# Half-wise layer norms, a whole-float32 router and idle TensorE products in a two-layer hybrid transformer kernel

## The chip, the cores and the metric

The kernel runs on one core of one Trainium2 chip. The time is the device time of one execution in microseconds (us), as a median of timed runs. Engines are called as in the profile: PE (TensorE matmul), PEld (its weight load), DVE (VectorE), ACT (ScalarE), POOL (GpSimd), SP (SyncE, which issues most DMAs).

## The reference

256 tokens of 1024 float32 features run through two layers. Each adds three branches in turn, with a layer norm after each; the cut below leaves the mixer and the attention to their names.

```python
x = layer_norm(x, ln_in_g, ln_in_b)
for l in range(2):
    h = hybrid_mixer(x, w_in[l], ...)            # retention and an RWKV7 scan, gated, w_out
    x = layer_norm(ALPHA * x + h, ln1_g[l], ln1_b[l])
    h = memory_cross_attention(x, mem, xa_wq[l], xa_wkv[l], xa_wo[l])
    x = layer_norm(ALPHA * x + h, ln2_g[l], ln2_b[l])
    h = grouped_moe(x, router_w, router_bias, moe_w_gate[l], moe_w_up[l], moe_w_down[l])
    x = layer_norm(ALPHA * x + h, ln3_g[l], ln3_b[l])

def grouped_moe(...):   # 16 experts in 4 groups of 4, width 512
    affinity = sigmoid(t @ router_w)
    choice = affinity + router_bias
    group_score = sum(top_k(choice by group, 2))
    best_group = argmax(group_score)
    idx = top_k(choice inside best_group, 2)
    wts = affinity[idx] / sum(affinity[idx])
    y = sum over e of combine[:, e] * ((silu(t @ w_gate[e]) * (t @ w_up[e])) @ w_down[e])
```

## The kernel before

All weights stream from memory in pieces of 1 MB on SP's queue into a ring of buffers (`slot`, `fetch`, `take`); a piece is loaded when its buffer's last reader is done. A Tile scheduler puts the instructions of each engine in an order once, when the program is built; `behind(ins)` asks for instructions to be issued after `ins`. Products of the dense parts take float32 numbers as a high and a low half: `split` (L135, L136) rounds the high one on ACT and subtracts the low one on DVE. `mm` (L127) is a product, `tr` (L131) a transpose on PE. The names in rows: `x` the tokens, `xT` their split transposes, `wh` the split weights, `raw`, `A`, `x` and `wh` the ring's buffers, `memT` the transposed memory tokens, `tp`, `acc`, `g` and `rk` PSUM tiles.

`layer_norm` (L284 to L301) takes statistics of both token blocks, finds the inverse root by three Newton steps on tiny tiles (L287 to L294), and writes x in halves of 512 features: subtract and scale (L297) for four pieces, then the last scale and offset (L301) for the same four. The transposes that follow on PE read x by columns of both blocks. In layer 0 the norm of the mixer and that of the attention have products on the memory tokens beside them (`spill_keys`, `spill_values`); in layer 1 those were done earlier, and PE has no other work there.

The expert part (`moe`) transposes x, splits it into `rx` (two buffers of `wh`), and `route` multiplies it with the split router as the stationary side (`g<-rx,rw`), copies to `big`, sums the halves with small products, and chooses experts in sixteen small DVE operations, from `aff` (L1048) to `sel` (L1075). Products with `sel` rank the tokens. `xs` is the split x for the gather, which multiplies it with a one-hot `oh`: half of the column blocks, then transposes of `oh` (`ohT`) and weights (`cws`), then the other half. Products of `xs` with a unit matrix start the output sums (`y`). An overflow flag is made from `rank` ahead of the gather. The expert stage then runs eight pairs of experts: gate, up, down.

## Time and profile before

| | |
|---|---|
| timed runs | 1311.02, 1313.77, 1318.09 us; median 1313.77 us |
| profiled execution | 1306.93 us, span 1304.6 us |
| PE busy | 1207.4 us (93%), 7648 instructions |
| DVE busy | 681.2 us (52%), 1446 instructions |
| ACT busy | 424.4 us (33%) |
| POOL busy | 81.9 us (6%) |
| HBM traffic | 253 GB/s over the span |

The shares are averages over stages with different limits. Layer 0 runs to about 673 us: norm and mixer, attention, router (404 to 452), experts (452 to 673). Layer 1 follows: mixer, its norm (965 to 986), attention, its norm (1041 to 1052), router and gather (1052 to 1072), experts (1072 to 1290), last norm. What a stage is worth is read from who ends PE's waits in it, and from the clock that PE was granted there.

### The profile page before, as it was taken

How to read it: one execution, taken by the hardware profiler on the slowest of the kernel's cores; microseconds unless marked ns; L12 is line 12 of the kernel's file. 1: busy time of each engine (PE TensorE's matmuls, PEld its weight loads, DVE VectorE, ACT ScalarE, POOL GpSimd, SP SyncE). 2: the span in 40 equal slices, each digit the busy share in tenths (PEclk: the TensorE clock that was granted, in tenths of full speed). 3: DMA queues.
4: the chain of work that ended last, by engine and by line, in shares of the span. 5: the costliest groups of instructions: out<-in, count | busy, mean ns of one | idle time of the engine just before them, and what ended most of it. 6: DMA issues, size and time to landing. Idle time of an engine off the chain costs nothing. (4 is left out here: it accounts for less than half of the span.)

```text
span 1304.6 us, 19215 instructions
## 1 busy us (share of the span) xinstructions
PE 1207.4 (93%) x7648; PEld 853.0 (65%) x7648; DVE 681.2 (52%) x1446; ACT 424.4 (33%) x689; POOL 81.9 (6%) x157
## 2 busy tenths in 40 slices
PE   8999998998999999999879999989979969999995
PEld 7887787996988744433339876879959744443332
DVE  6589787777548411101046797876875561110114
ACT  4556433453544301100025664234534220110000
POOL 0022222000000000000000113220000000000000
PEclk9999989999999999999999999899989979999998
DMA  9746222298635899999987453131987349999994
GB/s 324 260 143 192 79 75 76 81 372 283 232 129 207 310 396 403 399 395 402 400 331 229 155 182 106 43 108 66 346 295 282 109 162 382 400 396 400 402 396 200
DMA packets 189838, 331.04 MB, mean 254 GB/s; under 512 B 23152, under 2 KB 80880, under 8 KB 188720
## 3 DMA queue, kind: packets, MB, share of 16 engines
q1 hardware_dynamic: 187728, 324.51, 69.0%
q10 hardware_dynamic: 1728, 3.15, 0.7%
q0 software_dynamic: 288, 2.10, 0.4%
q8 instruction: 63, 1.03, 0.3%
q14 instruction: 31, 0.25, 0.1%
HBM read 321.86 MB, written 7.87 MB: 253 GB/s over the span
## 5 line engine op out<-in xcount | busy, mean ns | idle before, releaser
L136 DVE TENSOR_TENSOR wh<-raw,wh 128x1024 fp32r<-128x1024 f32 (+1 forms) x204 | 233.4, 1148 | 122.2 <-ACT wh L135 120.4
L135 ACT CAST wh<-raw 128x1024 fp32r<-128x1024 f32 (+1 forms) x204 | 199.8, 980 | 181.3 <-PE acc L127 166.5
L127 PE MATMUL acc<-xT,wh 128*128 128x256 f32 x1824 | 246.0, 290 | 2.3 <-DVE xT L136 1.5
L127 PEld LDWEIGHTS acc<-xT,wh 128*128 128x128 f32 x1824 | 228.5, 193 | 6.8 <-issue 2.1
L127 PE MATMUL g<-raw,xe 128*64 128x512 f32 x688 | 176.9, 596 | 1.4 <-DMA raw<-in_moe_w_up_dram 1.4
L127 PEld LDWEIGHTS g<-raw,xe 128*64 128x64 f32 x688 | 53.3, 137 | 95.4 <-issue 90.8
L127 PE MATMUL acc<-wh,xT 128*128 128x512 f32 x384 | 99.9, 405 | 2.7 <-DVE vg L557 2.7
L127 PE MATMUL g<-raw,hT 128*64 128x512 f32 x352 | 97.0, 596 | 1.8 <-DMA raw<-in_moe_w_down_dram 1.2
L1159 DVE TENSOR_TENSOR act<-act,g 128x512 f32<-128x512 f32 x16 | 11.0, 688 | 157.9 <-PE g L127 157.9
L1275 ACT ACTIVATE yh<-g,ws 128x512 fp32r<-128x512 f32 x32 | 22.0, 688 | 198.7 <-PE g L127 198.7
L1276 DVE SCALAR_TENSOR_TENSOR yl<-g,ws,yh 128x512 fp32r<-128x512 f32 x32 | 24.0, 751 | 114.6 <-ACT yh L1275 113.5
L127 PEld LDWEIGHTS acc<-wh,xT 128*128 128x128 f32 x384 | 70.2, 188 | 19.7 <-DVE vg L557 3.5
L127 PEld LDWEIGHTS g<-raw,hT 128*64 128x64 f32 x352 | 30.2, 137 | 55.5 <-issue 49.0
L127 PE MATMUL g<-wh,xe 128*64 128x512 f32 x184 | 56.5, 597 | 3.2 <-DMA wh<-in_moe_w_up_dram 3.2
L1206 DVE COPY xe<-g 128x512 f32<-128x512 f32 x16 | 11.1, 692 | 82.8 <-PE g L127 82.8
L127 PE MATMUL acc<-wh,memT 128*128 128x512 f32 x192 | 50.5, 414 | 0.3 <-ACT memT L135 0.3
L1147 ACT ACTIVATE act<-g 128x512 f32<-128x512 f32 x16 | 9.6, 598 | 124.9 <-PE g L127 124.9
L127 PE MATMUL acc<-memT,wh 128*128 128x256 f32 x384 | 46.9, 284 | 1.1 <-DVE wh L136 0.7
L127 PEld LDWEIGHTS acc<-memT,wh 128*128 128x128 f32 x384 | 46.3, 191 | 1.9 <-DVE wh L136 0.9
L127 PE MATMUL acc<-wh,mT 128*128 128x512 f32 x192 | 45.9, 398 | 0.8 <-DVE xr L406 0.7
L127 PE MATMUL acc<-wh,oT 128*128 128x512 f32 x192 | 45.7, 395 | 1.0 <-DVE x L406 0.8
L127 PE MATMUL acc<-ys,wh 128*128 128x256 f32 x384 | 45.1, 280 | 0.0
(292 smaller groups left out, 1691.3 us busy)
## 6 DMA issues: line engine op xcount, KB each, us to landing
raw<-in_w_in_dram SPq DMA_DIRECT2D x46, 1024.0 KB, 5.3
raw<-in_moe_w_down_dram SPq DMA_DIRECT2D x44, 1024.0 KB, 15.4
raw<-in_moe_w_gate_dram SPq DMA_DIRECT2D x43, 1024.0 KB, 13.9
raw<-in_moe_w_up_dram SPq DMA_DIRECT2D x43, 1024.0 KB, 13.9
raw<-in_xa_wkv_dram SPq DMA_DIRECT2D x16, 1024.0 KB, 10.1
wh<-in_moe_w_up_dram SPq DMA_DIRECT2D x15, 1024.0 KB, 14.2
A<-in_moe_w_down_dram SPq DMA_DIRECT2D x10, 1024.0 KB, 13.7
A<-in_moe_w_gate_dram SPq DMA_DIRECT2D x9, 1024.0 KB, 13.8
```

What stands on the lines that cost most here:

```text
L127: self.nc.tensor.matmul(out, lhsT, rhs, start=start, stop=stop, skip_group_check=True)
L135: self.nc.scalar.copy(out=hi, in_=src)
L136: (eng or self.nc.vector).tensor_sub(out=lo, in0=src, in1=hi)
L1147: nc.scalar.activation(act, ps, AF.Silu)
L1159: nc.vector.tensor_mul(out=act, in0=act, in1=ps)
L1206: nc.vector.tensor_copy(out=flat(t), in_=flat(ps))
L1275: nc.scalar.activation(yh, y[jc], AF.Copy, scale=ws)
L1276: nc.vector.scalar_tensor_tensor(out=yl, in0=y[jc], scalar=ws, in1=yh, op0=OP.mult, op1=OP.subtract)
```

## The change

- `layer_norm`: the first half of x gets its first scale before the Newton steps and its last scale right after them; the second half's first scales stand behind the first half's.
- `idle`: products of the unit matrix with constants, read by nobody, 10 behind w_out's last product in layer 1, 8 behind wo's in the last layer, 4 behind the logits there.
- In layer 1 the low halves of the first query weight piece are subtracted on POOL; those of the next two pieces stand behind the norm.
- Router: the transposed x is kept in whole float32 (`rx`, one buffer of `wh`), is the stationary side, and meets the whole router in sixteen products of 16 columns (eight blocks of features, two of tokens), straight into `z`. The choice takes twelve DVE operations.
- `xs` is split behind the last copy of `rx`, ahead of `aff`; the `y` products stand behind the logits.
- First gather: all column blocks first; transposes and weights of the lists behind the first gate product; the overflow flag (`beyond`) after the columns.

```diff
+W_NORM1, W_NORM2, W_ROUTE = 10, 8, 4
...
-    c["tie"] = np.broadcast_to((np.arange(4)[None] < np.arange(4)[:, None]).reshape(1, 16), (128, 16))
+    c["tie"] = np.broadcast_to((np.arange(4)[None] < np.arange(4)[:, None]).reshape(1, 16) * -1.2e-38, (128, 16))
...
-        self.nc.tensor.matmul(out, lhsT, rhs, start=start, stop=stop, skip_group_check=True)
+        self.product = self.nc.tensor.matmul(out, lhsT, rhs, start=start, stop=stop, skip_group_check=True)
+
+    def idle(self, n):
+
+        ps = self.pp.tile([128, 384], F32, name="warm", tag="b", bufs=4)
+        with self.behind(self.product):
+            for _ in range(n):
+                self.nc.tensor.matmul(ps, self.c["ident"], self.cst[:, 0:384], start=True, stop=True, skip_group_check=True)
...
-            self.split(flat(raw[:, j * n:j * n + n, :]), flat(hi), flat(lo))
+            self.split(flat(raw[:, j * n:j * n + n, :]), flat(hi), flat(lo), self.lower)
...
-            nc.vector.scalar_tensor_tensor(out=y, in0=e, scalar=1.5, in1=y, op0=OP.add, op1=OP.mult)
+            self.normed = nc.vector.scalar_tensor_tensor(out=y, in0=e, scalar=1.5, in1=y, op0=OP.add, op1=OP.mult)
+
         for j, s in enumerate(half):
             for tb in range(2):
-                nc.vector.scalar_tensor_tensor(out=out[:, tb, s], in0=src(tb, j), scalar=mv[:, tb, 0:1], in1=gb[:, 0, s],
-                                               op0=OP.subtract, op1=OP.mult)
-        for j, s in enumerate(half):
+                with self.behind(self.normed) if j else ExitStack():
+                    nc.vector.scalar_tensor_tensor(out=out[:, tb, s], in0=src(tb, j), scalar=mv[:, tb, 0:1], in1=gb[:, 0, s],
+                                                   op0=OP.subtract, op1=OP.mult)
             for tb in range(2):
                 self.normed = nc.vector.scalar_tensor_tensor(out=out[:, tb, s], in0=out[:, tb, s], scalar=y[:, tb], in1=gb[:, 1, s],
                                                              op0=OP.mult, op1=OP.add)
...
-            self.rw = const.tile([128, DK, 2, NE], F32R, name="rw")
+            self.rw = const.tile([128, DK, NE], F32, name="rw")
...
-            rwf = self.small.tile([128, DK, NE], F32, name="rwf", bufs=1)
-            nc.sync.dma_start(out=rwf, in_=a["router"])
-            self.split(rwf, self.rw[:, :, 0, :], self.rw[:, :, 1, :])
+            nc.sync.dma_start(out=self.rw, in_=a["router"])
...
         gb = self.project(a["w_out"][l], mT, xr, a["ln1_g"][l], a["ln1_b"][l])
+        if l:
+            self.idle(W_NORM1)
...
         for j in range(4):
-            with self.behind(normed) if j < NQ else ExitStack():
+
+            self.lower = nc.gpsimd if l and j == 0 else None
+            with self.behind(normed) if l and 0 < j < 3 else ExitStack():
                 ps = self.col(a["xa_wq"][l], j * 256, xT)
...
         gb = self.project(a["xa_wo"][l], oT, x, a["ln2_g"][l], a["ln2_b"][l])
+        if l + 1 == self.layers:
+            self.idle(W_NORM2)
         self.layer_norm(lambda tb, j: x[:, tb, j * 512:j * 512 + 512], gb, x)
...
-    def route(self, xT, rp, mo, lp):
+    def route(self, z, rp, mo):
...
-        ps = self.pp.tile([2 * NE, 256], F32, name="g", tag="b", bufs=4)
-        for k in range(DK):
-            w = self.rw[:, k].rearrange("p a e -> p (a e)")
-            for i in range(2):
-                self.mm(ps, w, xT[k // 2][i][:, k % 2, :], k == 0 and i == 0, k == DK - 1 and i == 1)
...
-        lg = big[0:2 * NE, 0:256]
-        nc.vector.tensor_copy(out=lg, in_=ps)
-        z = self.pp.tile([128, 2, NE], F32, name="g", tag="b", bufs=4)
-        for tb in range(2):
-            self.mm(z[:, tb, :], lg[:, tb * 128:tb * 128 + 128], c["id16"][0:2 * NE], True, True)
...
+        def ahead(v, n, at, count):
+            d = big[:, at:at + 16 * n].rearrange("p (a b c) -> p a b c", a=n, b=4)
+            nc.vector.tensor_tensor(out=d, in0=v[:, :, None, :].to_broadcast([128, n, 4, 4]), in1=v[:, :, :, None].to_broadcast([128, n, 4, 4]), op=OP.subtract)
+            nc.vector.scalar_tensor_tensor(out=d, in0=d, scalar=1.0, in1=tie.to_broadcast([128, n, 4, 4]), op0=OP.mult, op1=OP.is_gt)
+            nc.vector.tensor_reduce(out=count, in_=d, axis=AX.X, op=OP.add)
...
-        gt, eq = (big[:, i:i + 128].rearrange("p (a b c) -> p a b c", a=8, b=4) for i in (256, 384))
-        cj, ci = c4[:, :, None, :].to_broadcast([128, 8, 4, 4]), c4[:, :, :, None].to_broadcast([128, 8, 4, 4])
-        nc.vector.tensor_tensor(out=gt, in0=cj, in1=ci, op=OP.is_gt)
-        nc.vector.tensor_tensor(out=eq, in0=cj, in1=ci, op=OP.is_equal)
-        tie = c["tie"].rearrange("p (i j) -> p i j", i=4)[:, None, :, :].to_broadcast([128, 8, 4, 4])
-        nc.vector.tensor_mul(out=eq, in0=eq, in1=tie)
-        nc.vector.tensor_add(out=gt, in0=gt, in1=eq)
         before = R("before", (128, 8, 4))
-        nc.vector.tensor_reduce(out=before, in_=gt, axis=AX.X, op=OP.add)
+        ahead(c4, 8, 0, before)
...
-        m, best, top = R("m", (128, 2)), R("best", (128, 2, 4)), R("top", (128, 2))
-        nc.vector.tensor_reduce(out=m, in_=score, axis=AX.X, op=OP.max)
-        nc.vector.tensor_tensor(out=best, in0=score, in1=m[:, :, None].to_broadcast([128, 2, 4]), op=OP.is_equal)
-        nc.vector.tensor_mul(out=best, in0=best, in1=c["desc"][:, None, :].to_broadcast([128, 2, 4]))
-        nc.vector.tensor_reduce(out=top, in_=best, axis=AX.X, op=OP.max)
-        nc.vector.tensor_tensor(out=best, in0=best, in1=top[:, :, None].to_broadcast([128, 2, 4]), op=OP.is_equal)
+        ahead(score, 2, 128, worse)
...
+        return rank, cws, cw
+
+    def beyond(self, rank, cw, rp, lp):
...
-                rx = []
+                rx = self.wpool.tile([128, DK, 256], F32, name="rx", tag="wh", bufs=self.nhi)
+                z = self.pp.tile([128, 2, NE], F32, name="g", tag="b", bufs=4)
+
+                def logits(k):
+                    for i in range(k, k + 2):
+                        for tb in range(2):
+                            self.mm(z[:, tb, :], rx[:, i, tb * 128:tb * 128 + 128], self.rw[:, i, :], i == 0 and tb == 0, i == DK - 1)
+
                 for k in range(0, DK, 2):
                     ps = self.pp.tile([128, 2, 2, 128], F32, name="g", tag="b", bufs=4)
                     for j in range(2):
                         for tb in range(2):
                             self.tr(ps[:, j, tb, :], x[:, tb, (k + j) * 128:(k + j + 1) * 128])
-                    if k % 4 == 0:
-                        t = self.wpool.tile([128, 2, 2, 2, 256], F32R, name="rx", tag="wh", bufs=self.nhi)
-                    rx.append([t[:, k // 2 % 2, i] for i in range(2)])
-                    self.split(flat(ps), flat(rx[-1][0]), flat(rx[-1][1]))
-                rank, cws, cover, flag = self.route(rx, rp, mo, self.small)
-            xs = [self.xt.tile([128, 2, D], F32R, name=f"xs{i}", tag=f"xT{i}") for i in range(2)]
-            for tb in range(2):
-                self.split(x[:, tb, :], xs[0][:, tb, :], xs[1][:, tb, :])
-            if l + 1 < self.layers:
-                self.spill_values(l + 1, mem, 0)
-            self.ring = self.ring + [(self.wpool, "wh", self.nhi)] * self.nhi + [(self.xp, "x", 1)] + ([(self.aux, "A", 2)] * 2 if l + 1 < self.layers else [])
-            py.append([self.pp.tile([128, 512], F32, name="y", tag="c", bufs=2) for _ in range(2)])
-            for tb in range(2):
-                for jc in range(2):
-                    for i in range(2):
-                        self.mm(py[tb][jc], self.identr, xs[i][:, tb, jc * 512:jc * 512 + 512], i == 0, False)
-            lists, acts, ys = {}, {}, {}
-            step = self.gather(mo, 0, xs, rank, cws, lists)
-            self.finish(step)
+                    if k < DK // 2:
+                        nc.scalar.copy(out=flat(rx[:, k:k + 2, :]), in_=flat(ps))
+                    else:
+                        turned = nc.vector.tensor_copy(out=flat(rx[:, k:k + 2, :]), in_=flat(ps))
+                    if k >= 4:
+                        logits(k - 4)
+                logits(DK - 4)
+                logits(DK - 2)
+                chosen = self.product
+                if l + 1 == self.layers:
+                    self.idle(W_ROUTE)
+                xs = [self.xt.tile([128, 2, D], F32R, name=f"xs{i}", tag=f"xT{i}") for i in range(2)]
+                with self.behind(turned):
+                    for tb in range(2):
+                        self.split(x[:, tb, :], xs[0][:, tb, :], xs[1][:, tb, :])
+                rank, cws, cw = self.route(z, rp, mo)
+                if l + 1 < self.layers:
+                    self.spill_values(l + 1, mem, 0)
+                self.ring = self.ring + [(self.wpool, "wh", self.nhi)] * self.nhi + [(self.xp, "x", 1)] + ([(self.aux, "A", 2)] * 2 if l + 1 < self.layers else [])
+                py.append([self.pp.tile([128, 512], F32, name="y", tag="c", bufs=2) for _ in range(2)])
+                with self.behind(chosen):
+                    for tb in range(2):
+                        for jc in range(2):
+                            for i in range(2):
+                                self.mm(py[tb][jc], self.identr, xs[i][:, tb, jc * 512:jc * 512 + 512], i == 0, False)
+                lists, acts, ys = {}, {}, {}
+                first = self.gather(mo, 0, xs, rank, cws, lists)
+                next(first)
+                cover, flag = self.beyond(rank, cw, rp, self.small)
...
+                    if p == 0:
+                        self.finish(first)
...
-        for k in range(0, DK - 4, 2):
+        for k in range(0, DK - 4 if g else DK, 2):
             columns(k)
+            if g:
+                yield
+        if not g:
+            lists[g] = [xe, None, None]
             yield
...
-        for k in range(DK - 4, DK, 2):
+        for k in range(DK - 4 if g else DK, DK, 2):
             columns(k)
```

VectorE at the first norm of layer 1; `raw_8973` is a piece of wq, `lnm` the mean, `lny` and `lne` Newton's tiles. Before:

```order
L136 TENSOR_TENSOR wh<-raw_8973,wh 128x1024
L285 BN_AGGR lnm<-lnst 128x2
L297 SCALAR_TENSOR_TENSOR x<-xr,lnm,raw 128x512
L287 TENSOR_SCALAR lnv<-lnm 128x2
L297 SCALAR_TENSOR_TENSOR x<-xr,lnm,raw 128x512
L288 TENSOR_SCALAR lni<-lnv 128x2
L290 TENSOR_SCALAR lnn<-lnv 128x2
L297 SCALAR_TENSOR_TENSOR x<-xr,lnm,raw 128x512
L289 TENSOR_SCALAR lny<-lni 128x2
L297 SCALAR_TENSOR_TENSOR x<-xr,lnm,raw 128x512
L293 SCALAR_TENSOR_TENSOR lne<-lny,lnn 128x1 x2
```

And now, from the last Newton steps on:

```order
L301 SCALAR_TENSOR_TENSOR lny<-lne,lny 128x2
L300 SCALAR_TENSOR_TENSOR lne<-lny,lnn 128x1 x2
L301 SCALAR_TENSOR_TENSOR lny<-lne,lny 128x2
L309 SCALAR_TENSOR_TENSOR x<-x,lny,raw 128x512 x2
L306 SCALAR_TENSOR_TENSOR x<-xr,lnm,raw 128x512 x2
L309 SCALAR_TENSOR_TENSOR x<-x,lny,raw 128x512 x2
L143 TENSOR_TENSOR xT_8978<-tp,xT_8977 128x512 x2
L143 TENSOR_TENSOR wh<-raw_8966,wh 128x1024
```

The split of wq left the place ahead of the first scale; of the four first scales (L297, now L306) two stand between the last scales (L309) of the halves, and a split of wq follows the first split of xT.

TensorE from the attention's last product to the router's products in layer 1 (`oT` is the attention's output; L131 is now L138). Before:

```order
L127 MATMUL acc<-wh,oT_9300 128x512
L131 MATMUL g<-cst,x 128x128 x16
L127 MATMUL y<-xs_9644,identr 128x512
L127 MATMUL y<-xs_9645,identr 128x512
L127 MATMUL y<-xs_9644,identr 128x512
L127 MATMUL y<-xs_9645,identr 128x512
L127 MATMUL g<-rx,rw 32x256 x9
L127 MATMUL y<-xs_9644,identr 128x512
L127 MATMUL g<-rx,rw 32x256 x4
L127 MATMUL y<-xs_9644,identr 128x512
L127 MATMUL g<-rx,rw 32x256 x3
```

And now:

```order
L134 MATMUL warm<-cst 128x384 x8
L138 MATMUL g<-cst,x 128x128 x9
L127 MATMUL g<-rw,rx 128x16 x4
L138 MATMUL g<-cst,x 128x128
L127 MATMUL g<-rw,rx 128x16 x4
L138 MATMUL g<-cst,x 128x128 x6
L127 MATMUL g<-rw,rx 128x16 x8
L134 MATMUL warm<-cst 128x384 x4
L127 MATMUL y<-xs_9589,identr 128x512
```

Idle products (`warm`) came in ahead of the transposes and behind the logits, logits stand among the transposes, and the `y` products moved behind them.

TensorE inside the first gather of layer 1 (`raw_9699`, `raw_9701` are pieces of the experts' gate weights). Before:

```order
L127 MATMUL g<-oh,xs_9644 128x256 x2
L127 MATMUL g<-oh,xs_9645 128x256 x2
L131 MATMUL g<-cst,oh 128x128 x4
L127 MATMUL g<-cws,oh 64x2 x8
L127 MATMUL g<-oh,xs_9644 128x256 x2
L127 MATMUL g<-oh,xs_9645 128x256 x2
```

And now, at the end of the gather's columns:

```order
L127 MATMUL g<-oh,xs_9589 128x256 x2
L127 MATMUL g<-oh,xs_9590 128x256 x2
L127 MATMUL g<-ones,ovc 1x1
L127 MATMUL g<-raw_9699,xe 64x512
L127 MATMUL g<-raw_9701,xe 64x512
```

The transposes of `oh` and the products with `cws` left the middle of the gather; the flag's product (`ovc`) is followed at once by the gate products.

## Rows read from the trace of the kernel before

**Rows 1.** Windows: window and length (us), busy us (instructions) by engine, granted clock, DMA share, GB/s.
```profile
296.00:328.00 32.00, 27.38 (x120) 21.52 (x120) 22.95 (x42) 11.32 (x15) 0.00 (x0) 0.95 0.82 280
404.00:452.00 48.00, 47.80 (x348) 43.06 (x350) 32.30 (x74) 20.61 (x28) 0.00 (x0) 1.00 0.75 267
452.00:673.00 221.00, 215.76 (x1018) 84.58 (x1014) 29.96 (x45) 23.05 (x36) 0.00 (x0) 1.00 1.03 396
...
965.00:986.00 21.00, 12.38 (x76) 10.72 (x74) 14.99 (x34) 5.11 (x8) 0.00 (x0) 0.76 0.85 307
1041.00:1052.00 11.00, 3.97 (x18) 3.10 (x17) 10.27 (x28) 1.70 (x3) 0.00 (x0) 0.69 0.00 1
1052.00:1072.00 20.00, 13.89 (x95) 11.95 (x95) 10.72 (x36) 4.74 (x10) 0.00 (x0) 0.74 0.69 263
1072.00:1290.00 218.00, 213.47 (x1016) 84.06 (x1017) 29.32 (x45) 22.05 (x34) 0.00 (x0) 1.00 0.99 381
```

**Rows 2.** Timeline of PE at the start: start, length (us), instruction, count, [idle before, releaser].
```profile
24.95 11.43 PE L127 MATMUL acc<-memT,wh 128*128 128x256 f32 x94 [0.69 <-DVE wh L136]
...
43.70 2.50 PE L127 MATMUL acc<-xT,wh 128*128 128x256 f32 x19 [1.50 <-DVE xT L136]
```

**Rows 3.** Timeline of DVE at the same place.
```profile
41.67 0.17 DVE L458 TENSOR_SCALAR rest<-vec 128x4 f32<-128x4 f32 x1 [2.87 <-DMA vec<-in_vecs_dram]
```

**Rows 4.** Timeline of PE beside the first norm of layer 0.
```profile
314.40 0.90 PE L131 MATMUL tp<-cst,sg 128*128 128x128 f32 x4 [4.21 <-DVE memT L136]
```

**Rows 5.** Timeline of DVE at the same place.
```profile
313.66 0.68 DVE L136 TENSOR_TENSOR memT<-tp,memT 128x512 fp32r<-128x512 f32 x1
```

**Rows 6.** Timeline of PE after the first norm of layer 1.
```profile
974.33 2.20 PE L131 MATMUL tp<-cst,x 128*128 128x128 f32 x8 [8.59 <-DVE x L301]
...
985.97 1.99 PE L127 MATMUL rk<-kT,qT 128*128 128x256 f32 x8
```

**Rows 7.** Timeline of DVE in the first norm of layer 1.
```profile
964.05 1.23 DVE L136 TENSOR_TENSOR wh<-raw,wh 128x1024 fp32r<-128x1024 f32 x1 [1.57 <-ACT wh L135]
...
967.70 1.17 DVE L136 TENSOR_TENSOR wh<-raw,wh 128x1024 fp32r<-128x1024 f32 x1
...
970.39 0.75 DVE L297 SCALAR_TENSOR_TENSOR x<-xr,lnm,raw 128x512 f32<-128x512 f32 x1
```

**Rows 8.** Timeline of PE from the second norm of layer 1 to the experts.
```profile
1049.00 3.51 PE L131 MATMUL g<-cst,x 128*128 128x128 f32 x16 [7.03 <-DVE x L301]
...
1061.85 0.58 PE L127 MATMUL g<-sel,cst 128*128 128x16 f32 x2 [4.38 <-DVE sel L1075]
1062.26 0.59 PE L127 MATMUL g<-sel,ones 128*128 128x16 f32 x2
...
1064.88 3.78 PE L127 MATMUL g<-oh,xs 128*128 128x256 f32 x16
...
1071.92 2.37 PE L127 MATMUL g<-raw,xe 128*64 128x512 f32 x10
```

**Rows 9.** Timeline of DVE at the same place.
```profile
1048.19 2.74 DVE L301 SCALAR_TENSOR_TENSOR x<-x,lny,raw 128x512 f32<-128x512 f32 x4
...
1054.91 1.22 DVE L136 TENSOR_TENSOR xs<-x,xs 128x1024 fp32r<-128x1024 f32 x1
...
1057.73 0.18 DVE L1048 TENSOR_SCALAR aff<-aff 128x32 f32<-128x32 f32 x1 [1.28 <-ACT aff L1047]
```

**Rows 10.** Timeline of SP, the DMA queue, as the experts of layer 1 begin.
```profile
1075.60 0.88 SPq L150 DMA_DIRECT2D raw<-in_moe_w_down_dram  x2
```

**Rows 11.** Windows, as rows 1, of stretches granted half the clock.
```profile
830.09:840.33 10.24, 8.93 (x40) 8.73 (x41) 9.06 (x20) 2.96 (x3) 0.92 (x2) 0.50 0.20 33
...
1058.78:1069.02 10.24, 5.69 (x27) 5.60 (x28) 4.79 (x25) 0.81 (x2) 0.00 (x0) 0.50 0.72 287
```

**Rows 12.** One tile, `rm`: count, shortest/median/longest ns, first and last start, forms.
```profile
L569 DVE TENSOR_TENSOR rm<-rq,mixc x8: 426/928/962, 124.6 to 817.1; 128x256 f32<-128x256 f32 x8
```

**Rows 13.** Groups of POOL's instructions: busy us, mean ns, idle before and releasers.
```profile
L863 POOL TENSOR_TENSOR bkc<-bk,P 128x512 f32<-128x512 f32 x8 | 8.7, 1089 | 28.1 <-DVE bk L844 15.6 <-PE rk L131 12.3
```

More of the change, by code (lines that the diff above doesn't have):

```diff
@@ L34 @@
 NEXTRA = 4
-NQ = 0
 NM = 1
@@ L78, in _constants @@
     c["id64"] = np.concatenate([np.eye(64), np.eye(64)], 0)
-    c["id16"] = np.concatenate([np.eye(16)] * 8, 0)
-    c["desc"] = np.broadcast_to(np.arange(4, 0, -1)[None], (128, 4))
     gam = np.log(1.0 - 2.0 ** (-5.0 - np.arange(4.0)))
@@ L96, in pack @@
         return np.ascontiguousarray(np.concatenate([np.asarray(c[k], np.float32) for k in names], 1)), off
-    always = ["ident", "tri", "i64", "id16", "id64", "desc", "tie"]
+    always = ["ident", "tri", "i64", "id64", "tie"]
     return pack(always), pack([k for k in c if k not in always])
@@ L119, in __init__ @@
         self.ahead = []
+        self.lower = None
     def tap(self, name, ap):
@@ L1052, in route @@
         self.tap("choice", ch)
[L1054 to L1061 removed]
+        tie = c["tie"].rearrange("p (i j) -> p i j", i=4)[:, None, :, :]
+        def ahead(v, n, at, count):
[3 more added lines that the diff above has]
+            nc.vector.tensor_reduce(out=count, in_=d, axis=AX.X, op=OP.add)
+        c4 = ch.rearrange("p b (g e) -> p (b g) e", e=4)
         before = R("before", (128, 8, 4))
[L1063 removed]
+        ahead(c4, 8, 0, before)
         two, score = R("two", (128, 8, 4)), R("score", (128, 2, 4))
@@ L1066, in route @@
         nc.vector.tensor_reduce(out=score.rearrange("p b g -> p (b g)"), in_=two, axis=AX.X, op=OP.add)
-        m, best, top = R("m", (128, 2)), R("best", (128, 2, 4)), R("top", (128, 2))
-        nc.vector.tensor_reduce(out=m, in_=score, axis=AX.X, op=OP.max)
-        nc.vector.tensor_tensor(out=best, in0=score, in1=m[:, :, None].to_broadcast([128, 2, 4]), op=OP.is_equal)
-        nc.vector.tensor_mul(out=best, in0=best, in1=c["desc"][:, None, :].to_broadcast([128, 2, 4]))
-        nc.vector.tensor_reduce(out=top, in_=best, axis=AX.X, op=OP.max)
-        nc.vector.tensor_tensor(out=best, in0=best, in1=top[:, :, None].to_broadcast([128, 2, 4]), op=OP.is_equal)
+        worse = R("worse", (128, 2, 4))
+        ahead(score, 2, 128, worse)
         sel = R("sel")
         nc.vector.scalar_tensor_tensor(out=sel.rearrange("p b (g e) -> p (b g) e", e=4), in0=before, scalar=1.5,
-                                       in1=best.rearrange("p b g -> p (b g)")[:, :, None].to_broadcast([128, 8, 4]),
-                                       op0=OP.is_lt, op1=OP.mult)
+                                       in1=worse.rearrange("p b g -> p (b g)")[:, :, None].to_broadcast([128, 8, 4]),
+                                       op0=OP.is_lt, op1=OP.is_gt)
         rank = R("rank", pool=mo)
@@ L1093, in route, with R @@
         self.split(cw, cws[:, :, :, 0], cws[:, :, :, 1])
+        return rank, cws, cw
+    def beyond(self, rank, cw, rp, lp):
+        nc = self.nc
+        def R(name, shape=(128, 2, NE), pool=rp):
+            return pool.tile(list(shape), F32, name=name, bufs=1)
         over, ovc = R("over"), R("ovc", (128, 1))
@@ L1103, in route @@
         nc.vector.tensor_mul(out=cover, in0=over, in1=cw)
-        return rank, cws, cover, flag
+        return cover, flag
     def moe(self, l, x, mem):
```

## Prediction

> **What bounds the kernel now.** I read the table of stretches first [rows 1]. TensorE (PE) is busy for 47.80 of 48 us in the first router and for nearly all of both expert stages, where the weight stream also fills the DMA engines (share 1.03 and 0.99). An edit there moves nothing unless it takes work from PE or bytes from the stream. The second layer is different around its norms: from 965 to 986 PE is busy for 12.38 of 21 us, from 1041 to 1052 for 3.97 of 11, from 1052 to 1072 for 13.89 of 20. In these stretches the granted clock is a mean of 0.76, 0.69 and 0.74, so some 5.0, 3.4 and 5.2 us are lost to it on top of the standing still (twice those lengths were granted 1.2 GHz of 2.4). The reader should then look at who ends PE's waits: the layer norm's scale on VectorE (DVE) for 8.59 and 7.03 us [rows 6, 8], the choice of experts on DVE for 4.38 us [rows 8]. In layer 0 PE waits 4.21 us in its first layer norm, for a split of the memory tokens that queues behind the norm on DVE [rows 4, 5]. These waits are what the change can win: the four stretches.
>
> **The start.** The changed order puts the first tokens' transposes and their splits ahead of the two small operations on `vec`, which today hold DVE for 2.87 us until a DMA lands at 41.67 [rows 3]; the last splits of x run behind them and PE waits 1.50 us for them, after a gap of 0.69 us earlier [rows 2]. The 1.50 should go, and most of the 0.69, which stands where transposes now come earlier: I take -2.0. The bounds are 0 (the next weight piece is late instead) and -2.2, the sum of the two.
>
> **First norm of layer 0.** Before, all four subtract-and-scale operations (0.75 us each) stand on DVE ahead of Newton's steps, and the memory's split reaches DVE at 313.66 only [rows 5]. Now two of the four stand behind Newton, so the split can start about 2 x 0.75 = 1.5 us earlier and PE's wait falls from 4.21 to some 2.5 us: -1.7. PE then works through to the next transposes, so this is passed on. The mean clock of 0.95 over 32 us is 3.4 us at 1.2 GHz, which cost 1.7 us [rows 1]; it follows this wait and may vanish with it. Bounds -1.7 and -3.4; I take -2.7, nearer the second half, since the wait is cut by 40%. Five more splits of weights stand behind the second norm of this layer; products on memory tokens hide it, as PE at 47.80 of 48 us shows. Without that cover each would cost up to its 1.2 us.
>
> **Router and experts of layer 0.** The sixteen logits products are whole float32 and cost PE more than the sixteen they replace: a whole float32 product shows as two records. Those with `sel`, 16 columns wide, started 1061.85 and 1062.26, 0.41 apart at the low clock [rows 8], so about 0.21 at full: 16 x 0.21 = 3.4 us, against 16 x 0.12 = 1.9 (94 split products in 11.43 us [rows 2]), that is +1.5. Moving the lists' transposes and weights (four and sixteen products, about 1.4 us) behind the first gate product only shifts them. The expert stage has 221 - 215.8 = 5.2 us of PE waits and a full weight stream, which absorb 1.5: I take 0, the bound is +1.5.
>
> **First norm of layer 1.** Three things leave DVE ahead of the first transposes: a split of wq of 1.17 us in the middle of the norm, now behind it, and two of the four first scales, 2 x 0.75 [rows 7]. Half of these lie in the shadow of Newton's dependent small steps, as two of the four rows do today; so 1.17 + 0.6, about -1.7, gives the first transposes at 972.6 instead of 974.33. The second half of x is written about 1.1 us earlier too. The ten idle products stand between w_out and the transposes. Each has 384 columns of float32; four products of 256 columns (eight records) took 1.99 us [rows 6], 0.43 each with the last one's end taken off, so 1.5 x 0.43 = 0.65 us, together 6.5 us; the gap left is about 7, so they fit and delay nothing while the clock is full. If the clock then holds, the first query projection, which began at 1.2 GHz and ended at 985.97, ends at about 982.5: -3.5. If it doesn't, -1.7. A price the other way: wq's first piece is now split on GpSimd, two of 128x1024. Nearest rows: 1.09 us for 128x512 there, so 2.2 each [rows 13]. From when the cast is ready, before the DVE split at 964.05, they end by about 967, before the scales start. I take -2.75, since some of the clock or of GpSimd's time may bite. DVE slows beside GpSimd: one multiply of 128x256 took 426 ns at its shortest and a median of 928 [rows 12].
> [...]
>
> **Second norm and router of layer 1.** PE's transposes start at 1049.00 after 7.03 us [rows 8]; with two scales fewer ahead they start 1.1 to 1.4 us earlier, but x's second half is written as late as before, so only the logits count. DVE now copies two column pairs instead of subtracting four; the copy of `big` and PE's four summing products go. But both subtractions for `xs` (1.22 us each [rows 9]) move ahead of the first operation on `aff`, and whoever waits for `aff` waits for them. x ends at 1050.93 (1048.19 + 2.74 [rows 9]); seven transposes of 0.11 (half of 3.51 / 16 [rows 8]) and two copies of 0.7 (as long as the splits of [rows 5]) bring the last copy to 1052.7 or so. Two subtractions behind it end at 1055.1, if ScalarE's two casts were done by then; if they too wait for the last copy, each about as long as a subtraction, at 1056.2. The operation on `aff` follows there, against 1057.73: -1.5 to -2.6, I take -2.1. The sixteen operations from `aff` to `sel` span 1057.73 to 1061.85, 0.26 each; twelve remain: -1.0. Between `sel` and the first gather product the overflow flag's chain goes, -0.4. That is -3.5 without any help of the clock. Today the clock is at 1.2 GHz from 1058.78 to 1069.02 [rows 11], after PE stood still. Held at full, the three products with `sel` (six records, 0.21 apart) save 0.6. The first gate product follows the first gather product by 1071.92 - 1064.88 = 7.04 us; its first 16 gather products take 3.78 at the low clock, 0.22 each [rows 8]. Now 32 come first and the lists later: 32 x 0.22 = 7.0 at the low clock, 32 x 0.12 = 3.8 at full. So -3.5 with the clock lost, -3.5 - 0.6 - 3.2 = -7.3 with it held. The four idle products after the logits last 2.6 us, the y products 1.9; then PE still waits some 2 us for `sel` and 1 us for the one-hot. I take -5.25: clock lost in this wait, back within the gather.
> SP issues its next weights at 1075.60, after the first gate products have read their pieces [rows 10], and no bytes move from 1041 to 1052 [rows 1]. The stream, full from there (0.99), starts earlier by what the gate gains, and the end with it.
>
> **Last norm.** Two scales now stand behind Newton's steps, whose gaps they used to fill: +0.3 (0 to +0.6).
>
> **Sum.** -2.0 - 2.7 - 2.75 - 5.25 + 0.3 = -12.4 on the profiled 1306.93 us (span 1304.6), so 1294.5. That run is 6.8 us under the median of the three timed runs, 1313.77; I apply the same difference there: 1301.4.
>
> **Rivals.**
> *Clock not held.* The idle products fail to keep the full clock and only the order pays: -2.0 - 1.7 - 1.7 - 3.5 + 0.3 = -8.6, 1305.2. For it: ten products follow w_out, but DVE is what PE waits for, and a wait of 2 to 3 us after `sel` is left. Against: the other three waits shrink.
> *Held everywhere.* -2.0 - 3.4 - 3.5 - 7.3 + 0.3 = -15.9, 1297.9.
> *GpSimd in the way.* If a scale on DVE waits for a whole GpSimd split of 2.2 us in the first norm of layer 1 [rows 12, 13], the forecast gives that back: 1303.6. For it: the multiply at 928 ns. Against: the GpSimd splits have nearly ended when the two-input scales begin.
> *The stream sets the ends.* If the expert stages end when the weights do whenever PE starts, what is won ahead of them is swallowed: only +0.3 is left, 1314. For it: DMA shares of 1.03 and 0.99. Against: the stream stands still before the gate and restarts with it.
> *Slower: the scan's clock.* In the RWKV scan of each layer PE works in pieces of 64 columns with DVE in between, and one stretch of 10.24 us each was granted 1.2 GHz (830.09 to 840.33: PE busy 8.93, DVE 9.06) [rows 11]. Such a stretch costs up to 5.1 us. All of it starts earlier now and meets other pauses; three more stretches undo -12.4, four give +8.1 on the median, 1321.9. For it: the scan is DVE-paced. Against: its order is unchanged and only one stretch in each layer fell so far.
>
> **How the numbers follow.** Forecast 0.50, held everywhere 0.13, clock not held 0.17, GpSimd in the way 0.07, the stream 0.08, slower 0.05. The range takes the forecast's own bounds (route -3.5 to -7.3, start 0 to -2.2), both clock cases and GpSimd in the way: 1294 to 1311, leaving out the stream, the slower case and a tail below. Half a percent, 6.6 us, is about what a measurement of this kernel can tell from no change, so faster means under 1307.2: nearly all of the forecast and the held clock, two thirds of the clock lost, most of GpSimd in the way: 0.76. Same 0.19, slower 0.05.
>
> **What would show it.** In the changed profile: PE idle for 1.50 before the last x products gone; the wait for the memory's split at 2.5 us; the transposes after the first norm of layer 1 some 7.0 us after w_out's last product, granted clock 965 to 986 near 1; the first gate product 5 us earlier beyond the earlier shifts, counted from wo's last product (before: 1041.97 to 1071.92); SP's restart as much earlier. I am wrong if the expert stages lengthen by what the parts ahead of them gain, if idle products run into the transposes' start, or if a new stretch at 1.2 GHz appears.

## The result and the profile after

The changed kernel took 1296.46 us (median of four runs, 1293.89 to 1300.92) against 1312.39 us; the ratio is 0.9868 with a 95% interval of 0.9841 to 0.9895, so 14 to 21 us less. Its profiled execution took 1297.83 us, span 1296.1 us.

At the start the answer to [rows 2] is this (PE's timeline of the changed kernel; columns as there):

```profile
25.33 11.43 PE L127 MATMUL acc<-memT,wh 128*128 128x256 f32 x94 [0.92 <-DVE wh L143]
...
37.39 6.18 PE L127 MATMUL acc<-xT,wh 128*128 128x256 f32 x50
43.73 5.67 PE L127 MATMUL acc<-xT,wh 128*128 128x256 f32 x46 [0.15 <-DVE wh L143]
50.84 11.53 PE L127 MATMUL acc<-xT,wh 128*128 128x256 f32 x96 [1.45 <-DVE lora L644]
```

The wait of 1.50 us is gone, the other grew from 0.69 to 0.92, and a new one of 1.45 us, for `lora` on DVE, stands at 50.84. In the first norm of layer 0, the answer to [rows 4]:

```profile
315.11 0.85 PE L138 MATMUL tp<-cst,sg 128*128 128x128 f32 x4 [2.57 <-DVE memT L143]
```

The wait for the memory's split fell from 4.21 to 2.57 us. From the second norm of layer 1 to the experts, the answer to [rows 8]:

```profile
1038.02 5.33 PE L134 MATMUL warm<-cst 128*128 128x384 f32 x16
1044.23 0.41 PE L138 MATMUL g<-cst,x 128*128 128x128 f32 x2 [0.88 <-DVE x L309]
...
1046.88 0.30 PE L138 MATMUL g<-cst,x 128*128 128x128 f32 x1 [1.20 <-DVE x L309]
...
1050.09 3.59 PE L127 MATMUL g<-rw,rx 128*128 128x16 f32 x16 [0.26 <-DVE rx L1137]
1053.52 5.47 PE L134 MATMUL warm<-cst 128*128 128x384 f32 x8
1058.21 2.94 PE L127 MATMUL y<-xs,identr 128*128 128x512 f32 x8
1061.00 0.29 PE L127 MATMUL g<-sel,cst 128*128 128x16 f32 x2
...
1062.83 4.02 PE L127 MATMUL g<-oh,xs 128*128 128x256 f32 x32 [1.10 <-DVE cw L1090]
...
1066.90 4.08 PE L127 MATMUL g<-raw,xe 128*64 128x512 f32 x17
```

And DVE at the same place, the answer to [rows 9]; `sel` is written at 1056.87:

```profile
1043.33 1.41 DVE L309 SCALAR_TENSOR_TENSOR x<-x,lny,raw 128x512 f32<-128x512 f32 x2
...
1053.95 0.18 DVE L1050 TENSOR_SCALAR aff<-aff 128x32 f32<-128x32 f32 x1 [1.05 <-ACT aff L1049]
...
1056.87 0.19 DVE L1075 SCALAR_TENSOR_TENSOR sel<-before,worse 128x32 f32<-128x32 f32 x1
...
1061.77 0.19 DVE L1084 SCALAR_TENSOR_TENSOR rank<-g,sel 128x32 f32<-128x32 f32 x1 [4.26 <-PE g L127]
```

The gate starts 29.1 us after wo's last product; before, it took 30.3. `sel` is ready at 1057.06, but PE is still in idle products (8 records in 5.47 us) and then in the y products, and reads `sel` at 1061.00, 3.9 us late. The transposes come in two parts with 1.20 us of waiting between.

The six stretches of the argument, as differences between starts of PE products in each trace (us; the names of experiments are explained below). "q k" is the first product of query and keys, "gate" the first gate product, "last y" the last product into the output sums.

| stretch | before | after | a1 | a_shift | b256 | e_noidle | e_noroute | e_ln | best |
|---|---|---|---|---|---|---|---|---|---|
| layer 0, w_out's last to q k | 29.65 | 27.98 | 26.39 | 29.20 | 30.25 | 29.10 | 28.00 | 30.03 | 26.27 |
| layer 0, wo's last to gate | 47.81 | 47.06 | 47.05 | 50.20 | 47.83 | 50.08 | 47.06 | 47.59 | 46.95 |
| layer 0, gate to last y | 221.26 | 217.32 | 216.63 | 221.38 | 217.69 | 216.84 | 217.43 | 217.51 | 216.71 |
| layer 1, w_out's last to q k | 20.63 | 19.15 | 17.60 | 17.60 | 21.11 | 19.51 | 19.15 | 17.38 | 17.65 |
| layer 1, wo's last to gate | 30.34 | 29.11 | 29.07 | 29.06 | 30.56 | 27.07 | 27.48 | 25.76 | 29.71 |
| layer 1, gate to last y | 219.13 | 215.81 | 215.63 | 220.15 | 214.37 | 216.01 | 215.61 | 215.32 | 215.69 |

The largest gains, 3.9 and 3.3 us, are in the two expert stages, where no edit of the change was expected to move anything. The expert weights, of which no byte was taken away, come faster. Windows in the middle of layer 0's expert stage, before and after (columns as [rows 1]):

```profile
480.00:640.00 160.00, 157.01 (x754) 62.48 (x752) 22.07 (x33) 15.95 (x25) 0.00 (x0) 1.00 1.04 398
```

```profile
480.00:640.00 160.00, 159.15 (x768) 63.43 (x766) 22.08 (x33) 15.96 (x25) 0.00 (x0) 1.00 1.04 408
```

398 GB/s became 408, at the same share of busy DMA engines. What PE gained by it stands in its waits for weight pieces in layer 0's expert stage (what ended them; us in total, times, longest). Before:

```profile
PE g L127 <- DMA wh<-in_moe_w_up_dram: 1.6, 1, 1.6
PE g L127 <- DMA x<-in_moe_w_up_dram: 1.4, 1, 1.4
PE g L127 <- DMA raw<-in_moe_w_down_dram: 1.2, 2, 0.6
```

And after:

```profile
PE g L127 <- DMA raw<-in_moe_w_down_dram: 0.4, 1, 0.4
```

Together they fell from 4.2 to 0.4 us. Before, they lie late in the stage, from 622 us on.

### The profile page after: what moved, and what is told of

It reads as the page before. It is cut to its first block, busy times and chain, and to the rows that moved or that the text cites. A ratio compares the mean times of both kernels' runs of the same rounds, so it can differ in the third digit from the quotient of the medians.

```text
span 1296.1 us, 19329 instructions
## 1 busy us (share of the span) xinstructions
PE 1219.2 (94%) x7716; PEld 863.7 (67%) x7716; DVE 675.5 (52%) x1429; ACT 421.7 (33%) x684; POOL 86.9 (7%) x159
## 5 line engine op out<-in xcount | busy, mean ns | idle before, releaser
L143 DVE TENSOR_TENSOR wh<-raw,wh 128x1024 fp32r<-128x1024 f32 (+1 forms) x202 | 230.3, 1145 | 126.7 <-ACT wh L142 125.1
## 6 DMA issues: line engine op xcount, KB each, us to landing
raw<-in_moe_w_gate_dram SPq DMA_DIRECT2D x43, 1024.0 KB, 13.7
```

Of the source, the lines that this page charges most:

```text
L143: (eng or self.nc.vector).tensor_sub(out=lo, in0=src, in1=hi)
```

## The experiments

**Is it the kernel or the execution?** Two kernels are unchanged copies, side by side on one chip: b0 of the kernel before and a0 of the changed one.

> The kernel before, unchanged, beside the other three. In the profiles compared so far the expert weights land at one per 2.637 us before and one per 2.569 us after the change (pieces 16 to 80 of layer 0, 1 MB each). Theory S (the rate belongs to the execution or the chip, not to the kernel): the rate here is that of the changed kernel next to it within 0.5%. Theory K (the changed kernel streams faster): 2.64 here and 2.57 there again.

> The changed kernel, unchanged. Theory S: same rate of weights as the kernel before on this chip, and a gain of 5 to 8 us, what the norms and the router give (start -1.3, norm 1 of layer 0 -1.9, norms of layer 1 -2.5, router about 0). Theory K: 2.57 us per piece, a gain of 13 to 17 us as measured so far. In both, the products with sel start 3 to 4 us after sel is written, behind four idle products and the y products.

Pieces 16 to 80 of layer 0's expert weights landed one per 2.63 us in b0 and one per 2.59 us in a0 (2.63 and 2.58 in the first two profiles). The ratio of a0 to before was 0.9874 (0.9842 to 0.9906). The faster stream belongs to the kernel, so theory S and its 5 to 8 us fell.

**What in the kernel?** The change drops two tables from the constants and halves the router's tile, so every tile behind them starts at another address. In the built programs raw, wh and raw4 start 96 bytes beyond a multiple of 256 before and at a multiple after; x and A went from a multiple to 160 beyond; raw2 stays at 224 beyond. Three kernels move addresses and nothing else: no instruction and no order differs.

```diff
+            const.tile([128, 8], F32, name="gap")
```

That is b_shift, on the kernel before; a_shift and a_all are on the changed kernel:

```diff
+            const.tile([128, 152], F32, name="gap")
```

```diff
+            self.small.tile([128, 24], F32, name="gap", bufs=1)
+            ctx.enter_context(tc.tile_pool(name="edge", bufs=1, side="right")).tile([128, 56], F32, name="gap3")
...
+            aux.tile([128, 40], F32, name="gap2", bufs=1)
```

> The kernel before with one unused tile of 32 bytes per partition behind the constants; the instructions and their order are those of the kernel before. The weight buffers raw, wh and raw4 then start at multiples of 64 bytes (before: 32 beyond one), x and A no longer do. Theory A (the start address of the buffer sets how fast a weight piece lands): 2.57 us per expert piece instead of 2.64, both expert stages 3 to 4 us shorter (gate to last output product 217 to 218 us instead of 221), and 7 to 10 us less in all. Rival K' (the smaller router tiles or the earlier order of the change speed up the stream): 2.64 us and no change from before.

> The changed kernel with an unused tile of 608 bytes per partition behind the constants, instructions and order unchanged; raw, wh and raw4 start 32 bytes beyond a multiple of 64, as in the kernel before. Theory A: 2.64 us per piece, expert stages of 221 us, 7 to 10 us more than the changed kernel; what is left against before, 5 to 8 us, is what the change's own edits give. Rival K': 2.57 us and the changed kernel's time.

> The changed kernel with unused tiles placed so that all six kinds of weight buffers (raw, wh, raw4, raw2, A, x) start at multiples of 64 bytes; instructions and order unchanged. Theory A: 2.49 us per expert piece, as the pieces landing in such buffers already have; the expert stages shrink until PE is their bound (209 to 214 us busy), so 2 to 4 us each, 4 to 8 us less than the changed kernel: 1288 to 1292. Rival K': no change.

> All buffers at multiples of 64 bytes, and no idle products behind the logits of layer 1. Theory Q (they delay the products with sel): the first gate product of layer 1 comes 1 to 2 us earlier after wo's last product than with them (29.1 us), and since the stream no longer sets the end of the expert stage, the time falls by 1 to 2 us against the kernel with all buffers aligned. Rival: the same time.

a_shift lost most of the gain: 0.9943 (0.9913 to 0.9974) of before. b_shift gained nothing: 1.0028 (0.9993 to 1.0064); its expert stages, 222.9 and 221.1 us, are 1.7 and 2.0 longer in its profile than in that of before. So theory A fell in the form in which it was put, with 64 bytes: in b_shift the buffers stand at a multiple of 64, but 128 beyond one of 256, and x and A, at a multiple of 256 before, have left it. The same window in b_shift, a_shift and a_all:

```profile
480.00:640.00 160.00, 157.61 (x752) 62.15 (x748) 22.08 (x33) 15.69 (x25) 0.00 (x0) 1.00 1.04 394
```

```profile
480.00:640.00 160.00, 159.15 (x766) 63.37 (x762) 22.07 (x33) 15.34 (x24) 0.00 (x0) 1.00 1.04 398
```

```profile
480.00:640.00 160.00, 159.15 (x768) 63.50 (x766) 22.34 (x34) 15.35 (x24) 0.00 (x0) 1.00 1.04 412
```

The finer reading is the time between landings of expert pieces, sorted by where the buffer starts (bytes beyond a multiple of 256; median us, number of pieces; only pieces issued at least 3 us before the one ahead had landed):

| kernel | 0 | 32 | 96 | 128 | 160 | 224 |
|---|---|---|---|---|---|---|
| before | 2.48 (29) | | 2.70 (96) | | | 2.69 (45) |
| b_shift | | 2.70 (29) | | 2.70 (95) | | 2.67 (45) |
| a_shift | 2.48 (28) | | 2.70 (95) | | | 2.58 (45) |
| a1 | 2.50 (96) | | | | 2.59 (28) | 2.60 (46) |
| a_all | 2.55 (170) | | | | | |

Pieces overlap on the queue (in the profile before, medians of 13.7 to 15.4 us from issue to landing, with one landing per 2.63 us), so a buffer's neighbours may colour its number; but in each kernel that has both kinds the buffers at a multiple of 256 are the fastest. That gave a sharper theory, A256, and a kernel before with the change's own address classes. The 160 bytes didn't fit, so the router's staging tile moved into room that is free at the time.

```diff
+            const.tile([128, 40], F32, name="gap")
...
-            rwf = self.small.tile([128, DK, NE], F32, name="rwf", bufs=1)
+            rwf = mp.tile([128, DK, NE], F32, name="rwf", tag="yo")
```

> The kernel before with an unused tile of 160 bytes per partition behind the constants (paid for by letting the router's 512-byte staging tile share the room of yo; three small instructions at the very start move with it). raw, wh and raw4 now start at multiples of 256 bytes, as in the changed kernel; in the trial with 32 bytes they stood at 128 beyond one, and pieces took 2.70 us as before. Theory A256 (a piece lands faster where its buffer starts at a multiple of 256 bytes): 2.57 us per piece, expert stages 217 to 218.5 us, 7 to 10 us less than before. Rival (the address matters only in the changed kernel, say by another instruction's traffic): 2.64 to 2.66 us and no change.

```profile
480.00:640.00 160.00, 159.15 (x774) 63.46 (x772) 22.75 (x34) 15.94 (x25) 0.00 (x0) 1.00 1.04 408
```

408 GB/s, expert stages of 217.7 and 214.4 us, and a ratio of 0.9926 (0.9899 to 0.9954): 6 to 13 us less than before with none of the change's edits. The pieces in raw, wh and raw4 now land in 2.50 us (2.70 before), those in x and A in 2.62 (2.48 before). A256 holds. The three small instructions that moved with it lie in the first stage and can't shorten the expert stages. a_all streams at 412 GB/s, and yet its ratio, 0.9870 (0.9814 to 0.9927), can't be told from the changed kernel's 0.9868, where 4 to 8 us less were expected. Its expert stages are 0.7 and 1.0 us shorter than in the first profile of the changed kernel, and in layer 0 no shorter than in a1. The busy time of these windows doesn't tell why, since a_shift has the same 159.15 us at 398 GB/s. The waits do: in layer 0's expert stage PE waits 3.3 us for weight pieces in a_shift, 2.0 in b256, 0.4 in the changed kernel and 0 in a_all. With 408 GB/s little was left to gain. a_allnr (the same without the four idle products) was the same, 0.9886 (0.9828 to 0.9943): its gather ran slower (6.37 us for the 32 records against 4.02 in the changed kernel, with a mean granted clock of 0.71 up to the gate against 0.82) and the gate came after 29.0 us.

**The idle products.** e_noroute has `W_ROUTE` at 0, e_noidle all three counts.

```diff
-W_NORM1, W_NORM2, W_ROUTE = 10, 8, 4
+W_NORM1, W_NORM2, W_ROUTE = 10, 8, 0
```

> The changed kernel without the four idle products behind the logits of layer 1; the eighteen at the norms stay. Theory Q (they queue ahead of the y products and of the products with sel, and cost 3 to 4 us there at the low clock): sel is written as early as with them, its products follow within 0.3 us, the first gate product comes 3 us earlier, and the time falls by 2 to 4 us against the changed kernel. Theory C (they hold the clock for the gather): the gather's 32 products run at 1.2 GHz, 7 us instead of 4, and the time is the same or 1 to 3 us longer.

> The changed kernel without any idle products. Clock theory of the forecast: the first norm of layer 1 loses its clock again (mean 0.76 to 0.80 instead of 0.93 from there to the query projection), 1 to 2 us; the second norm loses 0 to 1 us; with the 3 us of the router's idle products coming back, the sum is -3 to +1 us against the changed kernel. Rival, the order alone gives all: within 1 us of the kernel without the four.

By the table, both reach the gate sooner, after 27.5 and 27.1 us instead of 29.1. Theory Q was right on the place, and C too on the clock: without them the 32 gather products of e_noroute ran partly at half the clock, 5.46 us against 4.02, and still it came out ahead there. (The profile gives the clock as a share of the full one; what the prediction and the expectations call 1.2 GHz is the share 0.50, at which gather products of 256 columns started 0.213 us apart in the kernel before, against 0.118 at 1.00.) At the first norm of layer 1 the ten products do what they should. PE's timeline of the changed kernel (a1) there, then of e_noidle:

```profile
960.59 6.61 PE L134 MATMUL warm<-cst 128*128 128x384 f32 x20
967.03 1.30 PE L138 MATMUL tp<-cst,x 128*128 128x128 f32 x8
...
977.96 1.35 PE L127 MATMUL rk<-kT,qT 128*128 128x256 f32 x5
```

```profile
972.75 2.20 PE L140 MATMUL tp<-cst,x 128*128 128x128 f32 x8 [5.95 <-DVE x L311]
...
985.92 1.35 PE L127 MATMUL rk<-kT,qT 128*128 128x256 f32 x5
```

8 transposes take 1.30 us instead of 2.20, the granted clock of the stretch is 1.00 instead of 0.74, and 19.5 us become 17.6. The gain is not always whole: in the first profile of the changed kernel and in e_noroute 3.4 us there were granted half the clock in spite of the ten products, and the stretch took 19.15 us. So idle products gave 0.4 to 1.9 us at the norm; at the router the kernels without the four are 1.6 to 2.0 us quicker (e_noidle has lost the eight at the second norm too), but a_allnr, with 17 us at half the clock there, is no quicker than a_all. In the whole time that can't be seen: e_noidle has 0.9895 (0.9846 to 0.9944) and e_noroute 0.9918 (0.9885 to 0.9952), the single runs of each kernel being up to 13 us apart, and both intervals overlap a0's. The three long runs of e_noroute (1303.75 to 1305.48 us) were granted a mean clock of 0.962 to 0.968, its two short ones 0.974 and 0.977; in which stretches they lost it is open.

**The norm in halves.** e_ln is the changed kernel with the old norm.

```diff
-                with self.behind(self.normed) if j else ExitStack():
-                    nc.vector.scalar_tensor_tensor(out=out[:, tb, s], in0=src(tb, j), scalar=mv[:, tb, 0:1], in1=gb[:, 0, s],
-                                                   op0=OP.subtract, op1=OP.mult)
+                nc.vector.scalar_tensor_tensor(out=out[:, tb, s], in0=src(tb, j), scalar=mv[:, tb, 0:1], in1=gb[:, 0, s],
+                                               op0=OP.subtract, op1=OP.mult)
+        for j, s in enumerate(half):
```

> The changed kernel with the layer norm of the kernel before (all four first scales ahead of Newton's steps). From w_out's last product to the first product of query and keys took 20.6 us before and 17.6 to 19.2 after the change in layer 1, 29.7 to 30.4 and 26.4 to 28.0 in layer 0. Theory H (half by half is what shortens these): 19 to 20.5 and 29.5 or more here, 2 to 3 us more than the changed kernel in all. Rival (the moved splits and the held clock do it): no more than 0.5 us lost in either.

In layer 0 theory H holds. The wait for the memory's split is back:

```profile
315.43 1.11 PE L138 MATMUL tp<-cst,sg 128*128 128x128 f32 x4 [4.24 <-DVE memT L143]
```

and the stretch takes 30.0 us. Part of that is the clock: 6.8 us of the stretch were granted 0.50, and a_shift and e_noidle, which keep the halves and have as much of it, take 29.1 to 29.2. In layer 1 the rival holds: 17.4 us, as with halves. And the router of layer 1 is quicker with the old norm than in any other kernel, 25.8 us. PE's timeline there:

```profile
1047.04 0.41 PE L138 MATMUL g<-cst,x 128*128 128x128 f32 x2 [1.96 <-DVE x L308]
1047.61 1.05 PE L138 MATMUL g<-cst,x 128*128 128x128 f32 x7 [0.16 <-DVE x L308]
...
1050.55 2.75 PE L127 MATMUL g<-rw,rx 128*128 128x16 f32 x24
1053.14 4.52 PE L134 MATMUL warm<-cst 128*128 128x384 f32 x8
1057.21 2.32 PE L127 MATMUL y<-xs,identr 128*128 128x512 f32 x8
1059.37 0.29 PE L127 MATMUL g<-sel,cst 128*128 128x16 f32 x2
...
1065.27 1.94 PE L127 MATMUL g<-raw,xe 128*64 128x512 f32 x8
```

The transposes start later (7.5 us after wo's last product, 6.4 in a1) but run without the wait in the middle, and 24 logits records take 2.75 us where 16 took 3.59 in the changed kernel. The granted clock of the whole stretch, changed kernel first:

```profile
1037.80:1066.90 29.10, 25.50 (x123) 19.09 (x121) 18.19 (x54) 5.01 (x9) 0.00 (x0) 0.82 0.47 172
```

```profile
1039.50:1065.30 25.80, 22.41 (x124) 16.88 (x122) 17.94 (x54) 4.94 (x9) 0.00 (x0) 0.93 0.54 196
```

0.82 against 0.93. The old norm was traced once here; the five profiles of the change's own order (the first, a0, a1, a_shift, a_all) reach the gate after 29.0 to 29.1 us. Whole times don't tell the two norms apart, 0.9885 (0.9838 to 0.9931) for e_ln and 0.9857 (0.9827 to 0.9888) for the changed kernel on the same chip.

**A version that should be better.** best has all buffers at multiples of 256, no idle products behind the logits, two behind each of the first two groups of logits, and the y products of layer 1 behind the first lists; a1 is the changed kernel again, beside it.

```diff
-W_NORM1, W_NORM2, W_ROUTE = 10, 8, 4
+W_NORM1, W_NORM2, W_ROUTE = 10, 8, 0
...
                         logits(k - 4)
+                        if l + 1 == self.layers:
+                            self.idle(2)
...
                         self.finish(first)
+                        if l + 1 == self.layers:
+                            start(self.product)
```

> The changed kernel with all weight buffers at multiples of 256 bytes, no idle products behind the logits but two behind each of the first two groups of logits, and the y products of layer 1 behind the first lists. From wo's last product to the first gate product took 30.3 us before, 29.1 after the change. Theory Q (what stands ahead of the products with sel on PE decides): 25.5 to 27 us, 2 to 3 us less than the changed kernel. Rival (the low clock that the removed work brings takes it back): 28 to 29 us, the same time.

> The changed kernel once more, beside the three others of this call, as what they are compared with on this chip. Both theories: 2.57 us per piece, 29.1 us from wo's last product to the first gate product, 1293 to 1301 us.

```profile
1057.03 0.61 PE L127 MATMUL g<-sel,cst 128*128 128x16 f32 x2 [3.43 <-DVE sel L1079]
...
1059.59 5.79 PE L127 MATMUL g<-oh,xs 128*128 128x256 f32 x32 [1.10 <-DVE cw L1094]
...
1065.43 1.94 PE L127 MATMUL g<-raw,xe 128*64 128x512 f32 x8
```

The rival held: PE now waits 3.43 us for `sel`, the gather runs slowly (5.79 us for 32 records), and the gate comes after 29.7 us. The ratio is 0.9904 (0.9878 to 0.9929), a1's 0.9857. No version here beats the changed kernel.

## Why the prediction was right, point by point

The time, 1296.46 against 1301.4, lies in the range, and the sign is right. The sum behind it is not, and that the total fits is in part luck: -12.4 us was meant to come from the edits, and by a_shift (the change with the old addresses) they give 1314.68 x 0.0057 = 7.5 us, 3 to 11 by its interval. The addresses, which no term had, give the rest: b256 alone has 1315.84 x 0.0074 = 9.7 us. Together 17; measured were 14 to 21. The bounds named in the prediction add up to -2.2 - 3.4 - 3.5 - 7.3 = -16.4, which is 1297.4; the measured time lies below that, and inside the range only because it was drawn down to 1294, for which no working is given. The rival "held everywhere" came nearest with 1297.9, but the clock was not held: in the first profile of the changed kernel it was granted 0.50 from 1049.30 to 1059.54.

- **"An edit there moves nothing unless it takes work from PE or bytes from the stream."** This step failed. PE did wait for the stream in both expert stages, as the prediction read from the DMA shares, but the stream's rate was taken as given. Smaller constants moved the buffers, and 4.6 and 3.5 us (before against a1) went. Neither the diff nor the order shows where a buffer starts. The rival in which the stream swallows all gains did not come: at its old rate, in a_shift, 7.5 us are still won.
- **The start, -2.0.** Mis-sized: the 151st product on x ends at 57.5 us in a1 and at 58.8 before, -1.3. At the 51st 2.8 us had been won (44.2 against 47.0); then PE waits 1.3 (a1) to 1.5 us for `lora`, a wait that no term had. In e_ln, with the old norm, the wait for the splits of x is back (1.53 us) and the 151st ends at 59.2. So the halves brought it, not the place of the `vec` operations by itself.
- **First norm of layer 0, -2.7.** Right in place, and the wait is 2.57 us as forecast (2.5); e_ln brings it back. The size goes with the clock. With 3.4 us at half the clock, as before, the stretch is 1.7 us shorter (first profile); in a1, where these are gone, 3.3, the bound that was named; in a_shift and e_noidle, with 6.8 us, only about 0.5.
- **Router of layer 0, 0.** wo to gate took 0.75 us less; in a_shift and e_noidle it took 2.3 to 2.4 more than before, both with half the clock for 6.8 us from 430 on.
- **First norm of layer 1, -2.75.** It was -1.5 (first profile, with 3.4 us at half the clock) and -3.0 (a1, with none): right. Its cause was read wrongly in part: by e_ln the two moved scales give nothing here, by e_noidle the clock gives up to 1.9; the remaining 1.1 may be the moved splits of wq, which no run took alone. The rival of GpSimd in the way fell. POOL's timeline of the changed kernel:

```profile
959.05 2.39 POOL L143 TENSOR_TENSOR wh<-raw,wh 128x1024 fp32r<-128x1024 f32 x1 [80.57 <-ACT wh L142]
961.79 2.39 POOL L143 TENSOR_TENSOR wh<-raw,wh 128x1024 fp32r<-128x1024 f32 x1 [0.35 <-ACT wh L142]
```

2.39 us each (2.2 was the estimate), over at 964.18, before the first two-input scale on DVE, so no run shows a scale that waits for a whole split, the 2.2 us of this rival:

```profile
964.80 0.73 DVE L306 SCALAR_TENSOR_TENSOR x<-xr,lnm,raw 128x512 f32<-128x512 f32 x1
```

- **Second norm and router of layer 1, -5.25.** Mis-sized: -1.2. The operation on `aff` came 16.2 us after wo's last product started, against 16.2 before, where -2.1 was forecast, since ScalarE had to wait for logits at a granted clock of 0.50 (16 records in 3.59 us); in e_ln, where they ran at the pace of the full clock (24 records in 2.75 us), it came after 14.4, -1.8. The twelve operations were nearly right: 2.9 us to `sel` instead of 3.8, -0.9 where -1.0 was forecast. Then failed the step "the four idle products last 2.6 us, the y products 1.9; then PE still waits some 2 us for `sel`": with the clock at 0.50 until 1059.54 they last 7.5 us, and `sel` waits 3.9 us for PE. The 32 gather products at full clock (4.02 us) and the lists behind the gate were as forecast.
- **Last norm, +0.3.** It did not come: from the last y product to the end of the span it took 13.3 us against 13.6.
- **Slower: the scan's clock.** In part it happened. In a1 one more stretch of the scan was granted half the clock, and from layer 0's last y product to the first product of layer 1's w_out it took 274.9 us against 270.1 before:

```profile
856.60:863.40 6.80, 5.52 (x39) 4.84 (x40) 5.41 (x39) 0.37 (x1) 0.00 (x0) 0.50 0.14 30
```

In the first profile of the changed kernel that stretch is absent and three (3.4, 6.8 and 3.4 us) stand in layer 0 instead, where before has one of 10.24. Nor is it shown to come from the change: b256, without any of its edits, has such a stretch from 867.62 to 874.45 and took 273.4 us, b0 took 271.6. These stretches come and go between executions of one kernel, as a1 and the first profile show for the changed one.

## What to carry to other kernels

Where a stream of weights bounds a stage, look at where its buffers start (here 398 or 408 GB/s): a table dropped from the constants can move them all, and an edit that is timed with such a move is not timed alone. Put an unused tile in to hold the addresses when an edit is measured. Idle work paid here where the engine would have stood still, at the first norm of layer 1 (0.4 to 1.9 us); in the queue ahead of the products with `sel`, where the clock had already dropped to 0.50, it made what was needed wait (`sel` for 3.9 us, behind the four and the y products).

## What the runs showed of the hardware that was not expected

Pieces of 1 MB landed in 2.48 to 2.50 us in buffers that start at a multiple of 256 bytes beside others that don't, in 2.55 us where all do, and in 2.67 to 2.70 us where none does. The 160 us of layer 0's expert stage shown above moved 394 GB/s with no buffer at a multiple, 398 with A and x there, 408 with raw, wh and raw4, 412 with all. A start 128 bytes beyond was as slow as one 32 or 96 beyond, 2.70 us each. Why a start at a multiple of 256 is the faster one (2.50 us in b256 against 2.70 in the kernel before) was not shown.
